# Products of 512 columns over both parts of a split activation, joined by accumulating transfers

## The chip, the cores and the metric

The kernel is one program on one core of a Trainium2 chip. The metric is the device time in microseconds (us). A measurement is the median of several runs. Beside them stands one execution that was profiled, and every row below is from that one.

## The reference, cut to what matters

One decoder layer over 512 tokens and 2048 features, in float32: a token mixer (a recurrent group and a differential-attention group), an output projection and a layer norm, and then the gated MLP, in which the change lies.

```python
hu = _causal_dwconv(jnp.einsum('bsd,df->bsf', x, w_up[i]), ffn_conv_w[i], ffn_conv_b[i])
g, u = jnp.split(hu, 2, axis=-1)
ffn = jnp.einsum('bsf,fd->bsd', jax.nn.gelu(g) * u, w_down[i])
```

`w_up` is 2048 x 11264: 44 tiles of 128 columns for g, 44 for u. The convolution is causal, of width 3, along the tokens, one filter for each column.

## The kernel before

**Split numbers.** TensorE multiplies in the type fp32r, which keeps fewer bits than float32. So every operand is split into a high part and a low part (`split`, lines 106 to 112: ScalarE copies the rounded high part, VectorE subtracts it), and a product is the sum of three matmuls (`mm3`, line 114): high by high, high by low, low by high.

**Pairs.** The first 4 tile pairs of the up projection (`PLAIN`) are computed plainly. Each of the other 40 is a `Pair`: one g tile and one u tile are seen as a 2 x 2 block matrix over the two halves of the features, the tokens as two halves of 256, and seven block products (`PRODUCTS`: p1, p5, p6, p2, p7, p3, p4) take the place of eight. The sums of weight blocks that they need are made by transfers that add to what stands in SBUF (`onto`, line 777, issued from GpSimd's queue) and by VectorE (lines 800 and 811). The sums of activation blocks are made once, in `forms` (line 727).

**Steps.** The loop of lines 916 to 923 counts steps; a pair's product number k (0 to 6) is its step k, and the pair after it begins 7 steps later. A step calls, for every pair in reach, `early` (evacuates an accumulator of the step before), `before` (loads, sums and splits of weights for later products: the blocks of a pair's p1, p5 and p6 are split at steps 5, 6 and 7 of the pair ahead of it), `late` (convolution, activation and the store of h to DRAM) and `product`. At a product TensorE makes 8 x 3 matmuls of 256 columns: three accumulators x, y, z of 256 columns serve the seven products, so p6 adds onto x only when `early` of step 1 has copied p1 out of it, p7 when that of step 3 has copied, p4 when that of step 5 has.

**Buffers.** `raw` tiles (weights as loaded, 4 KB for a partition) rotate through `RAW_UP` = 6 places, split weights through `W_BUFS` = 3, activations through `A_BUFS` = 62.

**Order.** The code names an engine for each operation, and a scheduler fixes the order on each engine when the program is built. On the chip each engine goes through its own order strictly: an instruction that waits holds up all behind it on that engine. The transfers that SyncE and GpSimd issue are two queues onto the same 16 DMA engines.

Of the kernel before, what the change touches and what calls it, by code (L numbers as in the profile page):

```python
# [10 lines left out]
F32 = mybir.dt.float32  # L11
F32R = mybir.dt.float32r
AF = mybir.ActivationFunctionType
ALU = mybir.AluOpType
# [33 lines left out]
NC_ = C_LQ + 4 * DH  # L48


A_BUFS = 62
T_BUFS = 12
RAW_BUFS = 3
RAW_UP = 6
W_BUFS = 3
TK = 0.65
LAG = 5.0
# [19 lines left out]
def f32(ap):  # L77
    return ap.bitcast(F32)
# [3 lines left out]
def trunk_kernel(ctx, tc, xT, w_qkg, w_v, gate_w, w_out0, w_out, w_up0, w_up, w_down, consts, out):  # L82
# [11 lines left out]
    def bank():  # L94
        return psum.tile([P, S], F32, tag="ps", bufs=8, name="ps")

    def a_tile(dt=F32R, name="a"):
        return act.tile([P, S], dt, tag="a", bufs=A_BUFS, name=name)

    def t_tile(dt=F32, name="t"):  # L100
        return tmp.tile([P, S], dt, tag="t", bufs=T_BUFS, name=name)
# [4 lines left out]
    def split(src, hi=None, lo=None, mk=a_tile):  # L106

        hi = mk(F32R, "hi") if hi is None else hi
        lo = mk(F32R, "lo") if lo is None else lo
        nc.scalar.activation(hi, src, AF.Copy)  # L110
        nc.vector.tensor_tensor(lo, src, f32(hi), ALU.subtract)  # L111
        return hi, lo

    def mm3(ps, w, x, first, last, onto=False):

        for n, (a, b) in enumerate(((w[0], x[0]), (w[0], x[1]), (w[1], x[0]))):
            nc.tensor.matmul(  # L117
                ps, a, b, start=first and n == 0, stop=last and n == 2, skip_group_check=onto
            )


# [432 lines left out]
    class Norm:  # L554
# [13 lines left out]
        def add(self, j, y, tok=slice(0, S), eng=nc.gpsimd):  # L568

            zs, qs = self.zs[:, tok], self.qs[:, tok]  # L570
            if j == 0:
                nc.scalar.activation(qs, y, AF.Square)
                eng.tensor_copy(zs, y)
            else:
                sq = t_tile(F32, "sq")[:, tok]
                nc.scalar.activation(sq, y, AF.Square)
                (nc.vector if j == KT - 2 else eng).tensor_tensor(zs, zs, y, ALU.add)  # L577
                eng = nc.vector if j == KT - 2 else nc.gpsimd
                eng.tensor_tensor(qs, qs, sq, ALU.add)
# [116 lines left out]
    def sides(z):  # L696
        return z[:, :HALF], z[:, HALF:]
# [29 lines left out]
    def forms(j):  # L727
        a, b = ys[j], ys[j + KT // 2]
        sub = nc.gpsimd.tensor_tensor
        t14, t23 = t_tile(F32, "t14"), t_tile(F32, "t23")  # L730
        (t1, t4), (t2, t3) = sides(t14), sides(t23)
        (b11, b12), (b21, b22) = sides(a), sides(b)
        sub(t1, b12, b11, ALU.subtract)
        sub(t2, t1, b22, ALU.subtract)
        sub(t4, t2, b21, ALU.add)
        sub(t3, b22, b12, ALU.subtract)
        h14, l14 = a_tile(F32R, "hi"), a_tile(F32R, "lo")
        nc.scalar.activation(h14, t14, AF.Copy, scale=-1.0)
        nc.vector.scalar_tensor_tensor(l14, t14, -1.0, f32(h14), ALU.mult, ALU.subtract)
        h23, l23 = split(t23)  # L740
        form["p1", j], form["p2", j] = sides(x1[j][0]), sides(x1[j + KT // 2][0])
        form["p3", j] = sides(x1[j + KT // 2][1])
        form["p5", j], form["p4", j] = zip(sides(h14), sides(l14))
        form["p6", j], form["p7", j] = zip(sides(h23), sides(l23))

    def conv(t, src, ti, *ds):
        for d in ds:
# [4 lines left out]
    def tap(src, ti):  # L752
        t = t_tile(F32, "cv")
        nc.scalar.activation(t, src, AF.Identity, scale=col(C_FW + 3 * ti + 2), bias=col(C_FB + ti))
        return t
# [11 lines left out]
    class Pair:  # L767
# [49 lines left out]

        def product(self, at):
            if at == 0:
                self.x, self.y, self.z = [bank()[:, :HALF] for _ in range(3)]  # L820
            name = PRODUCTS[at]
            ps = {"p5": self.y, "p3": self.y, "p2": self.z}.get(name, self.x)
            new = name in ("p1", "p5", "p2")
            hi, lo = self.w.pop(name)
            n = KT // 2
            for j in range(n):
                c = slice(j * P, (j + 1) * P)
                mm3(ps, (hi[:, c], lo[:, c]), form[name, j], new and j == 0, j == n - 1, not new)

        def early(self, at):  # L830
            copy, add = nc.scalar.activation, nc.vector.tensor_tensor
            a, b = slice(0, HALF), slice(HALF, S)
            if at == 1:
                self.cg = a_tile(F32, "cg")
                copy(self.cg[:, a], self.x, AF.Copy)
            elif at == 2:
                self.p5 = t_tile(F32, "p5")[:, :HALF]
                copy(self.p5, self.y, AF.Copy)
            elif at == 3:
                copy(self.cg[:, b], self.x, AF.Copy)  # L840
            elif at == 4:
                add(self.cg[:, a], self.cg[:, a], self.z, ALU.add)
            elif at == 5:
                self.cu = a_tile(F32, "cu")
                copy(self.cu[:, b], self.x, AF.Copy, scale=-1.0)
            elif at == 6:
                add(self.cg[:, b], self.cg[:, b], self.y, ALU.add)
                add(self.cu[:, b], self.cu[:, b], self.p5, ALU.subtract)
            elif at == 7:
                copy(self.cu[:, a], self.x, AF.Copy, scale=-1.0)  # L850

        def late(self, at):
            if at == 6:
                self.g = tap(self.cg, 2 * self.i)
                conv(self.g, self.cg, 2 * self.i, 1)
            elif at == 7:
                conv(self.g, self.cg, 2 * self.i, 2)
                self.u = tap(self.cu, 2 * self.i + 1)
            elif at == 8:
                conv(self.u, self.cu, 2 * self.i + 1, 1)  # L860
            elif at == 9:
                nc.scalar.activation(self.g, self.g, AF.Gelu_apprx_tanh)
            elif at == 10:
                conv(self.u, self.cu, 2 * self.i + 1, 2)
            elif at == 11:
                nc.vector.tensor_tensor(self.g, self.g, self.u, ALU.mult)
            elif at == 12:
                nc.sync.dma_start(hidd[self.i], self.g)

    pairs = [Pair(i) for i in range(PLAIN, FT)]  # L870
# [2 lines left out]
    def step(k, what, *reach):  # L873
        for n, pair in enumerate(pairs):
            if k - NP * n in range(*reach):
                getattr(pair, what)(k - NP * n)
# [39 lines left out]
    for k in range(last):  # L916
        step(k, "early", 1, 8)
        step(k, "before", -6, 5)
        step(k, "late", 6, 13)
        step(k, "product", 0, NP)  # L920
        ready({last - 5: 4, last - 3: 12, last - 2: 16}.get(k, 0))
        if k == last - 4:
            W.load()
    for k in range(last, last + 6):
        step(k, "early", 1, 8)
        step(k, "late", 6, 13)

    def down_blocks():
        while True:
# [155 lines left out]
```

## Time and profile before

| | us |
|---|---|
| median of 3 runs (2112.39 to 2113.21) | 2112.53 |
| the profiled execution | 2112.73 |
| its span, first to last instruction | 2111.0 |

The span is the stretch in which the profile shows instructions; 1.7 us of the execution lie around it. The profile's page gives the busy time of each engine; a busy TensorE (PE) is not TensorE at its best, since its matmuls are pipelined and overlap in the rows: what counts is the distance from one start to the next. Pairs are told by the copies of line 835, one for each of the 40.

### The profile page before, as it was taken

Reading aid. Unit: us, or ns where it says so; the run is one execution under the profiler, and the core shown is the slowest. Engines: PE = TensorE matmul, PEld = TensorE weight load, DVE = VectorE, ACT = ScalarE, POOL = GpSimd, SP = SyncE. Lnnn points to the kernel's source line nnn. Section 1 sums busy time; section 2 is a strip of 40 time slices with the busy share of each in tenths; the row PEclk is TensorE's granted clock in tenths of the full one; section 3 lists DMA queues with packets and bytes.
Section 4 is the critical chain, followed back from the end, with each engine's and each line's share of the span. In section 5 each row is a group of like instructions: output and inputs, shape, how many; then the busy total and the mean of one; then the engine's idle time right before and its main releaser. Section 6 shows DMA issues by size and latency. Waiting matters only on the chain.

```text
span 2111.0 us, 32632 instructions
## 1 busy us (share of the span) xinstructions
PE 2076.4 (98%) x13035; PEld 1882.6 (89%) x13035; DVE 1334.6 (63%) x2005; ACT 1004.4 (48%) x1644; POOL 240.7 (11%) x289
## 2 busy tenths in 40 slices
PE   9999999999999999999999999999999999999994
PEld 7888888888888899999999999999998888888894
DVE  6576635777335877777777777787776322443368
ACT  4475736666223645555555555555555222322144
POOL 1000000000222340000000000000000000010025
PEclk9999999999999999999999999999999999999997
DMA  6222222222433535666666666666669422333312
GB/s 217 95 80 85 81 95 71 85 98 93 152 118 120 180 86 156 170 167 173 169 175 167 168 175 171 167 175 165 171 163 329 161 93 97 125 110 100 100 50 81
DMA packets 92921, 286.67 MB, mean 136 GB/s; under 512 B 10080, under 2 KB 14176, under 8 KB 92768
## 3 DMA queue, kind: packets, MB, share of 16 engines
q1 hardware_dynamic: 81248, 242.63, 34.5%
q0 software_dynamic: 11520, 41.95, 11.1%
q8 instruction: 102, 1.67, 0.3%
q14 instruction: 51, 0.42, 0.1%
HBM read 264.62 MB, written 19.92 MB: 135 GB/s over the span
## 4 chain that ended last, share of the span: by engine, by line
PE 93%; DVE 4%; ACT 3%; issue 0%; DMA 0%; ACTq 0%; DVEq 0%
PE ps L117 91%; DVE acc L607 1%; PE ps L346 1%; PE ps L347 0%; ACT gt L455 0%; DVE acc L608 0%; PE ps L585 0%; PE ps L376 0%; DVE rstd L604 0%; DVE zs L577 0%; ACT s L358 0%; DVE y L607 0%; DVE y L608 0%; ACT a L461 0%; ACT L473 0%
## 5 line engine op out<-in xcount | busy, mean ns | idle before, releaser
L110 ACT ACTIVATE whi<-raw 128x512 fp32r<-128x512 f32 (+1 forms) x676 | 528.5, 804 | 900.4 <-PE ps L117 812.7
L111 DVE TENSOR_TENSOR wlo<-raw,whi 128x512 fp32r<-128x512 f32 (+1 forms) x676 | 614.3, 925 | 470.5 <-ACT whi L110 468.2
L117 PE MATMUL ps<-hi,whi 128*128 128x512 f32 (+1 forms) x2688 | 910.6, 339 | 0.0
L117 PE MATMUL ps<-hi,wlo 128*128 128x512 f32 (+1 forms) x2688 | 908.1, 338 | 1.2 <-DVE wlo L111 1.2
L117 PE MATMUL ps<-lo,whi 128*128 128x512 f32 (+1 forms) x2688 | 907.6, 338 | 0.0
L117 PEld LDWEIGHTS ps<-hi,wlo 128*128 128x128 f32 x2688 | 510.2, 190 | 56.1 <-DVE wlo L111 2.4
L117 PEld LDWEIGHTS ps<-hi,whi 128*128 128x128 f32 x2688 | 510.3, 190 | 53.1 <-ACT hi L110 0.3
L117 PEld LDWEIGHTS ps<-lo,whi 128*128 128x128 f32 x2688 | 510.4, 190 | 52.8 <-issue 0.5
L117 PE MATMUL ps<-x,whi 128*128 128x256 f32 x2176 | 396.9, 283 | 0.0
L117 PEld LDWEIGHTS ps<-x,whi 128*128 128x128 f32 x2176 | 339.5, 192 | 0.0
L117 PE MATMUL ps<-x,wlo 128*128 128x256 f32 x1088 | 308.0, 283 | 0.0
L117 PEld LDWEIGHTS ps<-x,wlo 128*128 128x128 f32 x1088 | 208.9, 192 | 0.0
L780 POOL DMA_DIRECT2D raw<-in_w_up x80 | 69.2, 964 | 767.8 <-DMA raw<-in_w_up 538.9
L956 POOL TENSOR_TENSOR acc<-acc,shift 128x512 f32<-128x512 f32 x16 | 23.5, 1478 | 437.7 <-ACT shift L566 296.6
L949 DVE SCALAR_TENSOR_TENSOR acc<-acc,ps 128x512 f32<-128x512 f32 x32 | 22.0, 687 | 66.7 <-PE ps L117 66.7
L748 DVE SCALAR_TENSOR_TENSOR cv<-cg,cst,cv 128x511 f32<-128x511 f32 x80 | 59.8, 747 | 1.4
L748 DVE SCALAR_TENSOR_TENSOR cv<-cu,cst,cv 128x511 f32<-128x511 f32 x80 | 59.5, 744 | 0.0
L117 PE MATMUL ps<-x,hi 128*128 128x256 f32 x256 | 49.4, 294 | 5.1 <-DVE x L111 3.3
L117 PE MATMUL ps<-hi 128*128 128x256 f32 (+1 forms) x176 | 51.9, 295 | 0.0
L117 PE MATMUL ps<-lo,hi 128*128 128x256 f32 (+1 forms) x176 | 51.5, 293 | 0.0
L117 PE MATMUL ps<-hi,lo 128*128 128x256 f32 (+1 forms) x176 | 51.5, 293 | 0.0
L800 DVE TENSOR_TENSOR raw<-raw 128x1024 f32<-128x1024 f32 x40 | 49.0, 1226 | 3.1 <-DMA raw<-in_w_up 1.8
(198 smaller groups left out, 1899.8 us busy)
## 6 DMA issues: line engine op xcount, KB each, us to landing
raw<-in_w_up SPq DMA_DIRECT2D x176, 512.0 KB, 4.1
raw<-in_w_down SPq DMA_DIRECT2D x88, 512.0 KB, 3.3
raw<-in_w_up POOLq DMA_DIRECT2D x80, 512.0 KB, 7.1
raw<-in_w_qkg SPq DMA_DIRECT2D x64, 512.0 KB, 3.5
raw<-in_w_out SPq DMA_DIRECT2D x32, 512.0 KB, 3.6
hidd<-cv SPq DMA_DIRECT2D x44, 256.0 KB, 4.2
hid<-hidd SPq DMA_DIRECT2D x44, 256.0 KB, 5.4
raw<-in_w_v SPq DMA_DIRECT2D x15, 512.0 KB, 4.3
```

What stands on the lines that cost most here:

```text
L110: nc.scalar.activation(hi, src, AF.Copy)
L111: nc.vector.tensor_tensor(lo, src, f32(hi), ALU.subtract)
L117: nc.tensor.matmul(ps, a, b, start=first and n == 0, stop=last and n == 2, skip_group_check=onto)
L346: nc.tensor.matmul(ps[:, :L], qs, k[c][:, :L], start=True, stop=False)
L607: sub.tensor_tensor(y, y, self.m[:, tok], ALU.subtract)
L748: nc.vector.scalar_tensor_tensor(t[:, d:], src[:, : S - d], col(C_FW + 3 * ti + 2 - d), t[:, d:], ALU.mult, ALU.add)
L780: nc.gpsimd.dma_start(self.raw[name], w_up[2 * (self.i - 2) + g][:, n * 1024 : (n + 1) * 1024], accum_op=ALU.add,)
L800: add(s2, self.raw["r21"], self.raw["r11"], ALU.add)
L949: nc.vector.scalar_tensor_tensor(acc[dt], acc[dt], 1.0 if c else ALPHA, ps, ALU.mult, ALU.add)
L956: nc.gpsimd.tensor_tensor(acc[d], acc[d], norm2.c, ALU.subtract)
```

## The change

A pair's matmul with a high half of weights now takes the high and the low part of the activation side by side, as one operand of 512 columns, and leaves high-by-high in the first 256 columns of the accumulator and high-by-low in the second (`mm2`). The matmul with the low half of weights adds onto the first 256 columns. So a block takes two matmuls, and the accumulators are 512 columns wide. `early` copies and adds at 512 columns, into `cg` and `cu` tiles of 1024 columns that have a ring of 3 of their own. Where a tile is complete, at steps 6 and 7, a transfer from GpSimd's queue adds its second half to its first (`accum_op=ALU.add`, SBUF to SBUF, 2 KB for a partition). `late` begins two steps later and reads the sum. `RAW_UP` goes from 6 to 5 and `A_BUFS` from 62 to 60. `forms` splits four quarters where it split two halves.

```diff
-A_BUFS = 62
+A_BUFS = 60
-RAW_UP = 6
+RAW_UP = 5
+    def mm2(ps, w, x, first, last, onto=False):
+        n = ps.shape[-1] // 2
+        steps = [(ps, w[0], x), (ps[:, :n], w[1], x[:, :n])]
+        for k, (o, a, b) in enumerate(reversed(steps) if last else steps):
+            nc.tensor.matmul(
+                o, a, b, start=first and k == 0, stop=last and k == 1, skip_group_check=onto
+            )
...
-        h14, l14 = a_tile(F32R, "hi"), a_tile(F32R, "lo")
-        nc.scalar.activation(h14, t14, AF.Copy, scale=-1.0)
-        nc.vector.scalar_tensor_tensor(l14, t14, -1.0, f32(h14), ALU.mult, ALU.subtract)
-        h23, l23 = split(t23)
+        for name, t in (("p5", t1), ("p4", t4)):
+            z = form[name, j] = a_tile(F32R, "hl")
+            hi, lo = sides(z)
+            nc.scalar.activation(hi, t, AF.Copy, scale=-1.0)
+            nc.vector.scalar_tensor_tensor(lo, t, -1.0, f32(hi), ALU.mult, ALU.subtract)
+        for name, t in (("p6", t2), ("p7", t3)):
+            form[name, j] = a_tile(F32R, "hl")
+            split(t, *sides(form[name, j]))
...
-                self.x, self.y, self.z = [bank()[:, :HALF] for _ in range(3)]
+                self.x, self.y, self.z = bank(), bank(), bank()
...
-                mm3(ps, (hi[:, c], lo[:, c]), form[name, j], new and j == 0, j == n - 1, not new)
+                mm2(ps, (hi[:, c], lo[:, c]), form[name, j], new and j == 0, j == n - 1, not new)
...
+            two = lambda z: z.rearrange("p (z t) -> p z t", z=2)
+            x, y, z = [two(k) for k in (self.x, self.y, self.z)]
             if at == 1:
-                self.cg = a_tile(F32, "cg")
-                copy(self.cg[:, a], self.x, AF.Copy)
+                self.cg = W.pool.tile([P, 2 * S], F32, tag="c", bufs=3, name="cg")
+                self.g2 = two(self.cg)
+                copy(self.g2[:, :, a], x, AF.Copy)
...
             elif at == 6:
-                add(self.cg[:, b], self.cg[:, b], self.y, ALU.add)
-                add(self.cu[:, b], self.cu[:, b], self.p5, ALU.subtract)
+                add(self.g2[:, :, b], self.g2[:, :, b], y, ALU.add)
+                nc.gpsimd.dma_start(self.cg[:, :S], self.cg[:, S:], accum_op=ALU.add)
+                add(self.u2[:, :, b], self.u2[:, :, b], self.p5, ALU.subtract)
             elif at == 7:
-                copy(self.cu[:, a], self.x, AF.Copy, scale=-1.0)
+                copy(self.u2[:, :, a], x, AF.Copy, scale=-1.0)
+                nc.gpsimd.dma_start(self.cu[:, :S], self.cu[:, S:], accum_op=ALU.add)
...
-            if at == 6:
-                self.g = tap(self.cg, 2 * self.i)
+            if at == 8:
+                self.g = tap(self.cg[:, :S], 2 * self.i)
+            elif at == 9:
                 conv(self.g, self.cg, 2 * self.i, 1)
-            elif at == 7:
+            elif at == 10:
                 conv(self.g, self.cg, 2 * self.i, 2)
-                self.u = tap(self.cu, 2 * self.i + 1)
+                self.u = tap(self.cu[:, :S], 2 * self.i + 1)
```

The scheduler's order on the engines, in the middle of the pairs. First GpSimd's queue. Before, it holds nothing but the two sums of weights of each pair, one after the other.

```order
L780 DMA raw_14346<-in_w_up 128x1024
L780 DMA raw_14515<-in_w_up 128x1024
L780 DMA raw_14580<-in_w_up 128x1024
L780 DMA raw_14749<-in_w_up 128x1024
L780 DMA raw_14814<-in_w_up 128x1024
```

In the changed kernel (where `onto` is line 792) a pair has four transfers: the sum onto the next pair's r21 (raw_10518), the sum onto its r11 (raw_10569), and then this pair's `cg` and `cu`.

```order
L792 DMA raw_10518<-in_w_up 128x1024
L792 DMA raw_10569<-in_w_up 128x1024
L865 DMA cg_10512<-cg_10512 128x512
L869 DMA cu_10615<-cu_10615 128x512
L792 DMA raw_10698<-in_w_up 128x1024
L792 DMA raw_10749<-in_w_up 128x1024
L865 DMA cg_10692<-cg_10692 128x512
L869 DMA cu_10795<-cu_10795 128x512
```

So the transfer that completes `cg` stands right behind the sum onto the next pair's r11, which waits until p1's block of that pair has been split out of the same tile.

Next ScalarE around the tap of g (line 754 before, 766 after: the first term of the convolution and its bias). Before, the tap of `cg` has only VectorE's addition ahead of it, and the copy that frees x for p6 (line 835, `cg_11701<-ps`) comes six instructions later.

```order
L110 ACTIVATE whi_11633<-raw_11473 128x1024
L754 ACTIVATE cv_11637<-cg_11467,cst_78 128x512
L110 ACTIVATE whi_11667<-raw_11603 128x1024
L850 ACTIVATE cu_11597<-ps_11440 128x256
L862 ACTIVATE cv_11637<-cv_11637 128x512
L754 ACTIVATE cv_11672<-cu_11597,cst_78 128x512
L110 ACTIVATE whi_11703<-raw_11540 128x1024
L835 ACTIVATE cg_11701<-ps_11674 128x256
```

In the changed kernel the tap waits for the transfer of `cg`, and the copy out of x (now line 851) stands right behind it.

```order
L110 ACTIVATE whi_10643<-raw_10518 128x1024
L868 ACTIVATE cu_10615<-ps_10493 128x2x256
L110 ACTIVATE whi_10668<-raw_10621 128x1024
L766 ACTIVATE cv_10702<-cg_10512,cst_78 128x512
L851 ACTIVATE cg_10692<-ps_10673 128x2x256
L110 ACTIVATE whi_10694<-raw_10571 128x1024
L854 ACTIVATE p5_10720<-ps_10674 128x512
L110 ACTIVATE whi_10723<-raw_10569 128x1024
```

The tap has moved from ahead of the split of p6's block (whi_11667) to behind it (whi_10668), and the copy that lets p6 begin (L851) is now the next instruction behind the tap.

Last VectorE over the same stretch. Before, from the addition that completes `cg` (line 847) on:

```order
L847 TENSOR_TENSOR cg_11467<-cg_11467,ps_11441 128x256
L111 TENSOR_TENSOR wlo_11634<-raw_11473,whi_11633 128x1024
L748 SCALAR_TENSOR_TENSOR cv_11637<-cg_11467,cst_78,cv_11637 128x511
L748 SCALAR_TENSOR_TENSOR cv_11637<-cg_11467,cst_78,cv_11637 128x510
L111 TENSOR_TENSOR wlo_11668<-raw_11603,whi_11667 128x1024
L811 TENSOR_TENSOR raw_11603<-raw_11603,raw_11540 128x1024
L748 SCALAR_TENSOR_TENSOR cv_11672<-cu_11597,cst_78,cv_11672 128x511
```

In the changed kernel, from the first convolution step behind the tap on (the numbers are those of ScalarE's rows above; line 760 is the convolution, 823 and 812 are the sums of weights, 858 adds z to `cg`):

```order
L760 SCALAR_TENSOR_TENSOR cv_10702<-cg_10512,cst_78,cv_10702 128x511
L823 TENSOR_TENSOR raw_10621<-raw_10621,raw_10571 128x1024
L111 TENSOR_TENSOR wlo_10695<-raw_10571,whi_10694 128x1024
L760 SCALAR_TENSOR_TENSOR cv_10702<-cg_10512,cst_78,cv_10702 128x510
L111 TENSOR_TENSOR wlo_10724<-raw_10569,whi_10723 128x1024
L760 SCALAR_TENSOR_TENSOR cv_10754<-cu_10615,cst_78,cv_10754 128x511
L760 SCALAR_TENSOR_TENSOR cv_10754<-cu_10615,cst_78,cv_10754 128x510
L885 TENSOR_TENSOR cv_10702<-cv_10702,cv_10754 128x512
L111 TENSOR_TENSOR wlo_10746<-raw_10621,whi_10745 128x1024
L858 TENSOR_TENSOR cg_10692<-cg_10692,ps_10675 128x2x256
L812 TENSOR_TENSOR raw_10801<-raw_10698,raw_10749 128x1024
L111 TENSOR_TENSOR wlo_10774<-raw_10666,whi_10773 128x1024
```

The next three rows there are the subtraction of p5 from `cu` (L866, 128x2x256), the split of the next pair's p1 (L111, wlo_10798<-raw_10749) and the addition that completes this pair's `cg` (L864). What moved: the convolution's first step, which waits for the transfer of `cg`, now stands ahead of a whole pair's work on VectorE, whose end releases the next such transfer.

## Rows read from the trace of the kernel before

**Rows 1.** Page, part 1: busy time, share of span, count by engine.
```profile
PE 2076.4 (98%) x13035; PEld 1882.6 (89%) x13035; DVE 1334.6 (63%) x2005; ACT 1004.4 (48%) x1644; POOL 240.7 (11%) x289
```

**Rows 2.** Stretch in the pairs: busy us (instructions) by engine, clock, DMA share, GB/s.
```profile
1200.00:1400.00 200.00, 200.00 (x1669) 200.00 (x1669) 153.90 (x169) 105.70 (x148) 17.27 (x20) 1.00 0.65 170
```

**Rows 3.** Tile cg: one line's executions, ns min/median/max, first and last start.
```profile
L835 ACT ACTIVATE cg<-ps x40: 362/365/367, 793.5 to 1579.7; 128x256 f32<-128x256 f32 x40
```

**Rows 4.** Timeline of TensorE: start us, duration us; 256 columns, then 512.
```profile
1200.06 0.28 PE L117 MATMUL ps<-lo,whi 128*128 128x256 f32 x1
1200.18 0.28 PE L117 MATMUL ps<-hi,wlo 128*128 128x256 f32 x1
...
1595.13 0.39 PE L117 MATMUL ps<-hi,whi 128*128 128x512 f32 x1
...
1598.98 0.39 PE L117 MATMUL ps<-hi,wlo 128*128 128x512 f32 x1
```

**Rows 5.** Timeline of VectorE, from the split of a next pair's p1 on.
```profile
1208.31 1.23 DVE L111 TENSOR_TENSOR wlo<-raw,whi 128x1024 fp32r<-128x1024 f32 x1 [1.65 <-ACT whi L110]
1209.46 0.42 DVE L848 TENSOR_TENSOR cu<-cu,p 128x256 f32<-128x256 f32 x1
...
1215.40 1.23 DVE L811 TENSOR_TENSOR raw<-raw 128x1024 f32<-128x1024 f32 x1
1216.54 0.74 DVE L748 SCALAR_TENSOR_TENSOR cv<-cu,cst,cv 128x511 f32<-128x511 f32 x1
1217.20 1.22 DVE L111 TENSOR_TENSOR wlo<-raw,whi 128x1024 fp32r<-128x1024 f32 x1
1218.34 0.74 DVE L748 SCALAR_TENSOR_TENSOR cv<-cu,cst,cv 128x510 f32<-128x510 f32 x1
1219.11 0.69 DVE L866 TENSOR_TENSOR cv<-cv 128x512 f32<-128x512 f32 x1
1219.84 1.23 DVE L111 TENSOR_TENSOR wlo<-raw,whi 128x1024 fp32r<-128x1024 f32 x1
```

**Rows 6.** Page, part 5: a VectorE operation of 512 columns on an accumulator.
```profile
L949 DVE SCALAR_TENSOR_TENSOR acc<-acc,ps 128x512 f32<-128x512 f32 x32 | 22.0, 687 | 66.7 <-PE ps L117 66.7
```

**Rows 7.** Timeline of ScalarE in the same pair.
```profile
1207.22 1.06 ACT L110 ACTIVATE whi<-raw 128x1024 fp32r<-128x1024 f32 x1 [1.82 <-PE ps L117]
...
1211.07 0.80 ACT L754 ACTIVATE cv<-cg,cst 128x512 f32<-128x512 f32 x1
...
1214.27 0.62 ACT L862 ACTIVATE cv<-cv 128x512 f32<-128x512 f32 x1
```

**Rows 8.** Timeline of GpSimd: transfers issued, two pairs.
```profile
1209.84 1.73 POOL L780 DMA_DIRECT2D raw<-in_w_up  x2 [18.43 <-DVE wlo L111]
1229.99 0.86 POOL L780 DMA_DIRECT2D raw<-in_w_up  x1 [18.43 <-DMA raw<-in_w_up]
1231.68 0.85 POOL L780 DMA_DIRECT2D raw<-in_w_up  x1 [0.83 <-issue]
```

**Rows 9.** Transfers issued at 1229.99, 1231.68, 1203.81, 1212.45 us: KB, us to landing.
```profile
raw<-in_w_up POOLq DMA_DIRECT2D x1, 512.0 KB, 5.2
...
raw<-in_w_up POOLq DMA_DIRECT2D x1, 512.0 KB, 8.3
...
raw<-in_w_up SPq DMA_DIRECT2D x1, 512.0 KB, 3.2
...
raw<-in_w_up SPq DMA_DIRECT2D x1, 512.0 KB, 8.1
```

**Rows 10.** Page, part 3: queue, packets, MB, share of 16 engines' span.
```profile
q0 software_dynamic: 11520, 41.95, 11.1%
```

**Rows 11.** Stretches around the one clock drop ahead of the last 30 us.
```profile
696.00:700.00 4.00, 2.24 (x19) 2.04 (x18) 4.00 (x6) 2.40 (x5) 4.00 (x6) 1.00 0.16 58
700.00:703.00 3.00, 0.74 (x6) 0.54 (x5) 3.00 (x4) 3.00 (x9) 3.00 (x5) 0.99 0.50 185
703.00:706.00 3.00, 1.97 (x9) 1.97 (x10) 3.00 (x6) 2.00 (x4) 1.57 (x2) 0.50 0.00 0
```

More of the change, by code (lines that the diff above doesn't have):

```diff
@@ L736, in forms @@
         sub(t3, b22, b12, ALU.subtract)
-        h14, l14 = a_tile(F32R, "hi"), a_tile(F32R, "lo")
-        nc.scalar.activation(h14, t14, AF.Copy, scale=-1.0)
-        nc.vector.scalar_tensor_tensor(l14, t14, -1.0, f32(h14), ALU.mult, ALU.subtract)
-        h23, l23 = split(t23)
[L741 to L744, printed above, removed]
+        form["p1", j], form["p2", j] = x1[j][0], x1[j + KT // 2][0]
+        form["p3", j] = x1[j + KT // 2][1]
+        for name, t in (("p5", t1), ("p4", t4)):
[6 more added lines that the diff above has]
+            split(t, *sides(form[name, j]))
     def conv(t, src, ti, *ds):
@@ L833, in early @@
             if at == 1:
-                self.cg = a_tile(F32, "cg")
-                copy(self.cg[:, a], self.x, AF.Copy)
+                self.cg = W.pool.tile([P, 2 * S], F32, tag="c", bufs=3, name="cg")
+                self.g2 = two(self.cg)
+                copy(self.g2[:, :, a], x, AF.Copy)
             elif at == 2:
-                self.p5 = t_tile(F32, "p5")[:, :HALF]
-                copy(self.p5, self.y, AF.Copy)
+                self.p5 = two(t_tile(F32, "p5"))
+                copy(self.p5, y, AF.Copy)
@@ L839, in early @@
             elif at == 3:
-                copy(self.cg[:, b], self.x, AF.Copy)
+                copy(self.g2[:, :, b], x, AF.Copy)
             elif at == 4:
-                add(self.cg[:, a], self.cg[:, a], self.z, ALU.add)
+                add(self.g2[:, :, a], self.g2[:, :, a], z, ALU.add)
             elif at == 5:
-                self.cu = a_tile(F32, "cu")
-                copy(self.cu[:, b], self.x, AF.Copy, scale=-1.0)
+                self.cu = W.pool.tile([P, 2 * S], F32, tag="c", bufs=3, name="cu")
@@ L846, in early @@
+                self.u2 = two(self.cu)
+                copy(self.u2[:, :, b], x, AF.Copy, scale=-1.0)
             elif at == 6:
-                add(self.cg[:, b], self.cg[:, b], self.y, ALU.add)
-                add(self.cu[:, b], self.cu[:, b], self.p5, ALU.subtract)
+                add(self.g2[:, :, b], self.g2[:, :, b], y, ALU.add)
+                nc.gpsimd.dma_start(self.cg[:, :S], self.cg[:, S:], accum_op=ALU.add)
+                add(self.u2[:, :, b], self.u2[:, :, b], self.p5, ALU.subtract)
@@ L857, in late @@
                 conv(self.g, self.cg, 2 * self.i, 2)
-                self.u = tap(self.cu, 2 * self.i + 1)
-            elif at == 8:
+                self.u = tap(self.cu[:, :S], 2 * self.i + 1)
+            elif at == 11:
                 conv(self.u, self.cu, 2 * self.i + 1, 1)
-            elif at == 9:
                 nc.scalar.activation(self.g, self.g, AF.Gelu_apprx_tanh)
-            elif at == 10:
+            elif at == 13:
                 conv(self.u, self.cu, 2 * self.i + 1, 2)
-            elif at == 11:
+            elif at == 14:
@@ L866, in late @@
                 nc.vector.tensor_tensor(self.g, self.g, self.u, ALU.mult)
-            elif at == 12:
+            elif at == 15:
                 nc.sync.dma_start(hidd[self.i], self.g)
@@ L918, in trunk_kernel @@
         step(k, "before", -6, 5)
-        step(k, "late", 6, 13)
+        step(k, "late", 8, 16)
         step(k, "product", 0, NP)
@@ L923, in trunk_kernel @@
             W.load()
-    for k in range(last, last + 6):
+    for k in range(last, last + 9):
         step(k, "early", 1, 8)
-        step(k, "late", 6, 13)
+        step(k, "late", 8, 16)
     def down_blocks():
```

## The prediction

> **What bounds the kernel now.** I read the engines' busy shares first, then the stretches, then the timelines of the engines in the pairs. TensorE is busy for 98% of the span [rows 1], and in the 200 us from 1200 on for all of them, at full clock (1.00, 2.4 GHz), while VectorE has 154 of 200 us and ScalarE 106 [rows 2]. The copy out of p1 starts first at 793.5 and last at 1579.7 us: 786.2 us for 39 distances, 20.16 us a pair [rows 3]. A matmul of 256 columns starts 0.120 us after the one before it [rows 4], and 7 products x 24 matmuls x 0.120 are 20.16 us. So a pair costs exactly its matmuls; nothing else shows.
>
> **What TensorE is spared.** Matmuls of 512 columns start 0.2265 us apart: 3.85 us for 17 distances, 1595.13 to 1598.98 [rows 4]. A block now costs 0.2265 + 0.120 = 0.3465 us where it cost 0.360, a product 2.77 us where it cost 2.88, a pair 19.40 us where it cost 20.16. That is 0.0135 us for each of 40 x 56 = 2240 blocks, 30 us in all, if TensorE stays the bound. That 512 and 256 columns alternate is not in the trace; the two distances are 256/2.4 and 512/2.4 ns plus the same 13 ns, so I add them up unchanged.
>
> The Trainium skill gives another price: its page "TensorE: Matmul & The Clock Gate" (Back-to-back issue gap) puts the isolated distance at the columns over 2.4 GHz plus some 2.5 ns, by which a matmul less would spare an estimated 2.5 x 2240 = 6 us. The rows show 13 ns where it has 2.5.
>
> **What is laid on the other engines.** Copies and additions of accumulators go from 256 to 512 columns. An addition from an accumulator is 0.69 us at 512 [rows 6]; three of them were 0.42 [rows 5], so VectorE gains 0.8 us a pair. ScalarE's five copies go to about the 0.62 us of a 512-column pass [rows 7], 1.3 us a pair. Both engines have the room as totals [rows 2]. Each matmul taken away also takes its weight load, which lies beside other matmuls. The four splits in `forms`, the scheduler's changed order in the attention, and two `a` tiles less I cost at nothing: TensorE covers them as it covers their likes now, and an engine that runs out there would cost a few us at most. One `raw` place less lets the loads of r11 and r12 start only when p2's and p7's blocks have been split, some three steps (8 us) ahead of their use; a load from SyncE lands in 3.2 us when alone [rows 9]. Hidden. So is the store of h, three steps later than now: only the down projection reads it.
>
> **The loop that the transfer of `cg` closes.** Here lies the cost. The order on the engines puts these in a ring, each waiting for the one before:
>
> 1. The tap of g on ScalarE waits for `cg` to land: 0.1 us of hand-over (my estimate; between VectorE and ScalarE rows show 0.03, to GpSimd 0.3), and 0.80 us itself [rows 7].
> 2. VectorE's first convolution step waits for the tap, and behind it, in order, stand 13 more operations up to the split of the next pair's p1. By distances between starts: four convolution steps at 0.66 (followed by another kind) to 0.77 (followed by what reads it), the product 0.73, the sum of weights and the splits 1.14 to 1.15, all from [rows 5]; two operations of 512 columns at 0.65, a little under the 0.69 of [rows 6]. That is 0.66 + 0.66 + 0.75 + 0.77 + 0.73 + 5 x 1.14 + 0.09 (the last split to its end) + 2 x 1.15 + 2 x 0.65 = 13.0 us. With every one hidden 0.09 us under the next it is 12.6, with none 13.65 (the durations added).
> 3. That split ends, and 0.30 us later (1209.54 to 1209.84, [rows 5, 8]) GpSimd issues the sum onto r11, which had waited for it. `cg`'s addition ends 0.65 us after the split, while GpSimd is still issuing, so `cg` goes out right behind.
> 4. The sum onto r11 lands 5.2 us after issue when nothing else moves [rows 9]. The load onto the next r21 goes out just then (when p5's block is split, 1.2 us after `cg`'s addition) and moves beside its end; I take 5.5, and 5.7 as the high end, both estimates.
> 5. `cg`'s transfer moves half the bytes and comes after it in the same queue. Alone: 41.95 MB of such sums took 11.1% of 16 engines' 2111 us [rows 10], 80 of them, so 2.93 us each and 1.46 for half. Sharing with a load: of two sums issued at 1229.99 and 1231.68 [rows 8] the first landed 5.2 us later and the second 8.3 [rows 9], 4.8 us after the first, half of it 2.4; or all 4.8, if the 128 rows count and not their bytes. That the two queues hold each other up shows in SyncE's load, 3.2 us alone and 8.1 beside two such sums [rows 9]. Since r21's load is about, I take 2.4.
>
> Sum: 0.1 + 0.8 + 13.0 + 0.3 + 5.5 + 2.4 = **22.1 us** around the ring, between 20.4 (0.05 + 0.8 + 12.6 + 0.3 + 5.2 + 1.46) and 25.5 (0.2 + 0.8 + 13.65 + 0.3 + 5.7 + 4.8). All of it is longer than TensorE's 19.40, and even the lower end is longer than the 20.16 of now. TensorE is drawn into it since the copy that frees x for p6 stands right behind the tap on ScalarE: it should stand still for 2.7 us ahead of every p6. The other way around, over TensorE, is shorter: tap 0.8, copy 0.6, p6, p2 and p7 8.3, copy 0.6, split 1.06 and 1.23 [rows 5, 7] come to 12.6 against 13.8. Before, the tap waited for VectorE's addition alone, and no transfer stood between the pairs' work.
>
> A pair then costs 22.1 - 20.16 = 1.94 us more, over 39 distances 76 us. At the end, the last `cu` goes through a transfer ahead of its tap, and splits for the down projection stand behind that tap on ScalarE; between 0 (hidden) and 6 us (issue to landing of such a transfer and its tap): I take 3. From the profiled execution's 2112.73, which is the median of the runs to within 0.2 us: 2112.7 + 76 + 3 = **2192 us**.
>
> **Rivals.**
>
> *The transfer of `cg` does not queue behind the sum onto r11 (faster).* Then it is issued 0.3 + 0.86 us [rows 8] after the split of p1 and lands as a sum of half the bytes would alone, 5.2 - 1.46 = 3.7 us later: 0.1 + 0.8 + 13.0 + 1.2 + 3.7 = 18.8, under 19.40, and TensorE stays the bound. 2112.7 - 30 + 3 = 2086 us. It turns at a landing 4.3 us after issue. Against it: the second of two sums never landed near the first in [rows 8, 9], though each alone takes 5.2. I give it 0.13.
>
> The Trainium skill would lean to this one: "DMA: Bandwidth & Descriptors" (Anatomy of one DMA) has 2.0 us plus the bytes over 436 GB/s for a transfer from GpSimd's queue, an estimated 2.6 us for 256 KB, and so a ring of some 18 us. By the same rule the 512 KB of [rows 9] would take 3.2 us, and they took 5.2: an adding transfer is dearer than the rule.
>
> *TensorE's clock drops in the gaps (slower still).* The one drop ahead of the end came after TensorE had been idle for 1.76 and 2.26 of 7 us, and 0.50 (1.2 GHz) was granted afterwards [rows 11]. One gap of 2.7 us in 22 is smaller, and I think the clock holds. At half the clock p6 alone would take 2.8 us more, the way over TensorE 15.4 instead of 12.6, which is 1.6 over VectorE's 13.8: 23.7 us a pair, 2254 us. With p2 slowed as well it would be 26.5 us, 2363 us. I give it 0.10.
>
> *The ring is short after all.* With every term near its low end a pair stays within 20.4 to 21.1 us, and the time within 2125 to 2152: 0.08. Within 0.2% of now 0.03, since that needs a ring between 20.0 and 20.2.
>
> **How the numbers follow.** My forecast, a ring of 21.1 to 24 us, has 0.66, and its own range is 2152 to 2265. With the short ring below it and half of the clock's case above it, 2125 to 2300 holds 8 in 10; the faster case, no change and the dearer half of the clock's case stay out. 0.2% (4 us) is about what a measurement of this kernel tells from no change. Faster 0.13, the same 0.03, slower 0.84.
>
> **What the changed profile would show.** The distance between the first and the last copy of line 851 over 39: 22.1 by me, 19.4 by the first rival. The tap of `cg` on ScalarE idle ahead of it, released by a transfer, in every pair; TensorE idle ahead of p6, released by that copy; GpSimd's `cg` issues landing 7 to 8 us after issue (under 4.3 by the rival); VectorE without idle time from the convolution to the split of p1. Starts of matmuls 0.227 and 0.120 us apart show the relief. I am wrong if the tap finds `cg` landed, or if another instruction than the tap starts the wait.

## The result and the profile after

| | us |
|---|---|
| changed kernel, median of 4 runs (2212.78 to 2218.88) | 2215.52 |
| kernel before, median of 4 runs (2111.99 to 2113.21) | 2112.46 |
| ratio, 95% interval | 1.0488 [1.047, 1.0506] |
| the profiled execution and its span | 2212.78, 2210.9 |

The change costs 103 us, where 79 were forecast; between the two profiled executions it is 100.1, since the profiled execution of the changed kernel is its fastest. The page of the changed kernel, part 1, answers to [rows 1]: TensorE has 2240 matmuls less and is busy for 95% instead of 98%.

```profile
PE 2093.0 (95%) x10795; PEld 1780.0 (81%) x10795; DVE 1348.5 (61%) x2021; ACT 1045.9 (47%) x1660; POOL 309.1 (14%) x369
```

The stretch of [rows 2]: TensorE has 184 of 200 us instead of 200, and the mean clock is no longer 1.00. VectorE does less in 200 us than before (142 us for 154), since fewer pairs pass; ScalarE does as much (105 us), since each of its copies is longer.

```profile
1200.00:1400.00 200.00, 183.56 (x1004) 157.65 (x1005) 141.79 (x153) 105.04 (x135) 31.09 (x36) 0.97 0.72 175
```

The tile `cg` in the changed kernel, as in [rows 3]: first the executions of the copy of line 851 and of the tap, then what the instructions on `cg` waited for and who waited for them (us, times), then the transfers' time to landing.

```profile
L851 ACT ACTIVATE cg<-ps x40: 574/576/601, 793.8 to 1674.4; 128x512 f32<-128x512 f32 x40
...
  DMA cg<-cg: 183.1, 39
...
  DVE cv L760: 171.2, 40
...
  PE ps L127: 78.6, 39
...
DMA to landing us min/median/max: 6.6/7.5/9.7
```

From 793.8 to 1674.4 are 880.6 us over 39 distances: 22.58 us a pair, 2.42 more than before, 94.4 in all. Behind the last copy the span has 536.5 us where it had 531.3, 5.2 more. With 0.3 us at the start that is the 100 us. And the three waits form a chain: the tap waits for the transfer in 39 pairs, VectorE's convolution for the tap, TensorE for the copy behind the tap, 2.0 us each time (78.6 over 39).

One pair follows, engine by engine. ScalarE's timeline (start us, duration us, in brackets the idle time and what ended it):

```profile
1222.64 0.81 ACT L766 ACTIVATE cv<-cg,cst 128x512 f32<-128x512 f32 x1 [4.08 <-DMA cg<-cg]
1223.36 0.58 ACT L851 ACTIVATE cg<-ps 128x512 f32<-128x512 f32 x1
...
1244.84 0.81 ACT L766 ACTIVATE cv<-cg,cst 128x512 f32<-128x512 f32 x1 [4.93 <-DMA cg<-cg]
```

VectorE's timeline; the first two rows are of the pair before it, the rest of this one, to compare with [rows 5]:

```profile
1212.01 0.69 DVE L866 TENSOR_TENSOR cu<-cu,p 128x512 f32<-128x512 f32 x1 [0.37 <-ACT cu L862]
1212.96 1.23 DVE L111 TENSOR_TENSOR wlo<-raw,whi 128x1024 fp32r<-128x1024 f32 x1 [0.25 <-ACT whi L110]
...
1223.49 0.75 DVE L760 SCALAR_TENSOR_TENSOR cv<-cg,cst,cv 128x511 f32<-128x511 f32 x1 [3.66 <-ACT cv L766]
...
1235.07 1.22 DVE L111 TENSOR_TENSOR wlo<-raw,whi 128x1024 fp32r<-128x1024 f32 x1
1236.21 0.68 DVE L864 TENSOR_TENSOR cg<-cg,ps 128x512 f32<-128x512 f32 x1
```

GpSimd's issues in the same pair, as in [rows 8], the sum onto the next r11 first and `cg` behind it:

```profile
1236.58 0.86 POOL L792 DMA_DIRECT2D raw<-in_w_up  x1 [12.42 <-DVE wlo L111]
1237.18 1.14 POOL L865 DMA_DIRECT2D cg<-cg  x1
```

And the landing of these two, KB and us from issue, as in [rows 9]:

```profile
raw<-in_w_up POOLq DMA_DIRECT2D x1, 512.0 KB, 5.5
...
cg<-cg POOLq DMA_DIRECT2D x1, 256.0 KB, 7.6
```

The reader can walk the ring: tap to convolution 0.85 us (1222.64 to 1223.49), VectorE without a gap to the end of the split of p1 at 1236.29, which is 12.80, 0.29 to GpSimd's issue at 1236.58, 5.5 to the landing of the sum, and `cg` at 1237.18 + 7.6 = 1244.8, 2.7 behind it; the next tap starts at 1244.84. Together 22.20 us, with TensorE and ScalarE waiting in turn.

### The profile page after: what moved, and what is told of

It reads as the page before. It is cut to its first block, busy times and chain, and to the rows that moved or that the text cites. A ratio compares the mean times of both kernels' runs of the same rounds, so it can differ in the third digit from the quotient of the medians.

```text
span 2210.9 us, 28573 instructions
## 1 busy us (share of the span) xinstructions
PE 2093.0 (95%) x10795; PEld 1780.0 (81%) x10795; DVE 1348.5 (61%) x2021; ACT 1045.9 (47%) x1660; POOL 309.1 (14%) x369
## 4 chain that ended last, share of the span: by engine, by line
PE 52%; DMA 21%; issue 13%; DVE 8%; ACT 4%; POOL 1%; POOLq 0%; ACTq 0%; DVEq 0%; SPq 0%
PE ps L117 50%; DMA cg<-cg 13%; DMA raw<-in_w_up 8%; DVE wlo L111 3%; ACT cv L766 1%; DVE raw L823 1%; POOL raw L792 1%; PE ps L127 1%; DVE acc L617 1%; PE ps L356 1%; ACT gt L465 0%; PE ps L357 0%; DVE acc L618 0%; PE ps L595 0%; ACT s L368 0%
## 5 line engine op out<-in xcount | busy, mean ns | idle before, releaser
L111 DVE TENSOR_TENSOR wlo<-raw,whi 128x512 fp32r<-128x512 f32 (+1 forms) x676 | 611.8, 922 | 415.1 <-ACT whi L110 413.7
L127 PE MATMUL ps<-hl,whi 128*128 128x512 f32 x1280 | 489.2, 414 | 78.6 <-ACT cg L851 78.6
L117 PE MATMUL ps<-hi,whi 128*128 128x512 f32 (+1 forms) x1408 | 548.6, 390 | 0.8 <-ACT hi L110 0.7
L117 PE MATMUL ps<-hi,wlo 128*128 128x512 f32 (+1 forms) x1408 | 545.9, 388 | 3.4 <-DVE wlo L111 3.4
L117 PE MATMUL ps<-lo,whi 128*128 128x512 f32 (+1 forms) x1408 | 545.5, 387 | 0.9 <-DVE lo L111 0.9
L127 PEld LDWEIGHTS ps<-hl,whi 128*128 128x128 f32 x1280 | 251.2, 196 | 138.1 <-ACT cg L851 90.9
L127 PE MATMUL ps<-x,whi 128*128 128x512 f32 x960 | 349.2, 398 | 0.0
L127 PE MATMUL ps<-hl,wlo 128*128 128x256 f32 x1280 | 343.0, 289 | 0.0
L117 PEld LDWEIGHTS ps<-hi,wlo 128*128 128x128 f32 x1408 | 264.4, 188 | 59.2 <-DVE wlo L111 5.3
L117 PEld LDWEIGHTS ps<-hi,whi 128*128 128x128 f32 x1408 | 264.5, 188 | 53.7 <-ACT hi L110 1.6
L127 PEld LDWEIGHTS ps<-hl,wlo 128*128 128x128 f32 x1280 | 252.5, 197 | 13.4
L968 DVE SCALAR_TENSOR_TENSOR acc<-acc,ps 128x512 f32<-128x512 f32 x32 | 21.9, 685 | 65.7 <-PE ps L117 65.7
```

The source lines that it names most:

```text
L117: nc.tensor.matmul(ps, a, b, start=first and n == 0, stop=last and n == 2, skip_group_check=onto)
L127: nc.tensor.matmul(o, a, b, start=first and k == 0, stop=last and k == 1, skip_group_check=onto)
L968: nc.vector.scalar_tensor_tensor(acc[dt], acc[dt], 1.0 if c else ALPHA, ps, ALU.mult, ALU.add)
```

## The experiments

Each was compared with the kernel before; ratios are to it. "A pair" is the distance between the first and the last of the 40 copies out of p1, over 39. The twelve were not planned at once: the second four follow from what the first showed, the last four from the second.

**1. Neither part nor transfer** (`e_none`).

```diff
-                nc.gpsimd.dma_start(self.cg[:, :S], self.cg[:, S:], accum_op=ALU.add)
-                nc.gpsimd.dma_start(self.cu[:, :S], self.cu[:, S:], accum_op=ALU.add)
```

> Both SBUF-to-SBUF transfers are left out, so the products of the weights' high halves with the low parts of x1 are missing from the output; all else stays as in the changed kernel. If the ring of tap, VectorE chain, sum onto r11 and transfer of cg sets the pair's time, it is gone: TensorE is the bound at 19.40 us a pair, no gap ahead of p6, full clock, 2083 to 2088 us. If the 512-column copies and additions, the rawu pool of five places or the alternation of 512 and 256 columns cost something of their own, that part stays: a pair above 19.6 us, and the time above 2092 us. If the alternation gives no relief at all, 20.16 us a pair and 2112 us.

2105.63 us, 0.9968 [0.9958, 0.9979], 19.79 us a pair:

```profile
L851 ACT ACTIVATE cg<-ps x40: 598/598/602, 795.1 to 1567.1; 128x512 f32<-128x512 f32 x40
```

The ring is gone, and with it the gaps of 2 us and the drops of the clock within the pairs. Five places for raw weights, wider copies and wider additions cost next to nothing here: TensorE stands idle for 0.04 us a pair. But the relief is smaller than forecast: 0.37 us a pair, not 0.76. Nor does the end get all of it: behind the last copy are 539.0 us, 7.7 more than before.

**2. The transfers are issued, and nobody reads what they add** (`e_unread`).

```diff
-                self.g = tap(self.cg[:, :S], 2 * self.i)
+                self.g = tap(self.cg[:, S:], 2 * self.i)
...
-                self.u = tap(self.cu[:, :S], 2 * self.i + 1)
+                self.u = tap(self.cu[:, S:], 2 * self.i + 1)
```

(`conv` reads the same half. This half is what the transfer takes from: it holds high-by-low alone. So what the output lacks here, and in experiment 6, is the first half, high-by-high and low-by-high, and not the low parts' products, as the two expectations have it. The waits are those that they describe.)

> Both transfers are issued as in the changed kernel, but the taps and convolutions read the other half of cg and cu (the source of the transfer), so nobody waits for a landing except for the place in the pool; the low parts' products are missing from the output. By the ring it is the waiting that costs: 2083 to 2090 us, 19.4 to 19.6 us a pair, as without transfers. By the rival that the transfers' traffic costs (it holds up the loads of weights in the other queue, and the splits with them), it stays above 2150 us. In between, 2095 to 2150, both have a part.

2192.08 us, 1.0379 [1.0364, 1.0395], 21.91 us a pair. Read by itself this says that the waiting for `cg` is not the cause, and that the rival is right. The trace names another wait. VectorE's timeline, where line 812 is the addition of r21 and r11:

```profile
1045.89 1.23 DVE L812 TENSOR_TENSOR raw<-raw 128x1024 f32<-128x1024 f32 x1 [5.07 <-issue]
...
1050.51 1.22 DVE L111 TENSOR_TENSOR wlo<-raw,whi 128x1024 fp32r<-128x1024 f32 x1
...
1066.86 1.23 DVE L812 TENSOR_TENSOR raw<-raw 128x1024 f32<-128x1024 f32 x1 [1.78 <-issue]
```

The load onto the next r21 (SyncE, issued at 1051.76) and the sum onto it (GpSimd, 1059.51), KB and us to landing:

```profile
raw<-in_w_up SPq DMA_DIRECT2D x1, 512.0 KB, 7.2
...
raw<-in_w_up POOLq DMA_DIRECT2D x1, 512.0 KB, 7.3
```

This is a second ring. A pair takes five raw tiles (r21, r11, r12, s2, r22), and with five places the next r21 gets the place of this one. It is free when p5's block is split out of it, at 1051.73; the load lands at 1058.9, the sum is issued at 1059.51 and lands at 1066.8, the addition starts at 1066.86, and 5.8 us later the next split of p5 ends. That is 21.0 us around, above the 19.7 that TensorE needs. The mean of 21.9 holds more than this pair: 15 of the 39 distances hold a stretch at half the clock and are 24.47 us on average, the other 24 are 20.31. How the excess divides between the ring and the clock that its gaps cost is not shown.

**3. No sum onto r11** (`e_no11`).

```diff
                 add(s2, self.raw["r21"], self.raw["r11"], ALU.add)
-                self.onto("r11", (1, 0))
```

> The sum onto r11 is left out, so p7's weights are those of one block alone and the output differs there; cg's transfer is then first in GpSimd's queue when it is issued. If cg is late because it queues behind the sum onto r11, it lands 3.5 to 4.5 us after issue instead of 7.5, the ring is 18.8 to 19.6 us, and the time 2083 to 2095 us. If an adding transfer of 256 KB is slow by itself whatever stands ahead of it, it lands after 6 us or more, the ring stays at 21 us or more, and the time above 2150 us.

2105.43 us, 0.9967 [0.9954, 0.998], 19.78 us a pair. The transfers of `cg` in this run:

```profile
DMA to landing us min/median/max: 3.6/3.6/7.6
```

An adding transfer of 256 KB lands 3.6 us after issue when it is first in the queue, and 7.5 behind a sum of 512 KB. So the ring over `cg` is the queue's doing. The time missed the expected 2083 to 2095 us by the smaller relief alone. The second ring opened as well: the load and the sum of r21, beside `cg` and `cu` but with no sum onto r11, now took

```profile
raw<-in_w_up SPq DMA_DIRECT2D x1, 512.0 KB, 4.0
...
raw<-in_w_up POOLq DMA_DIRECT2D x1, 512.0 KB, 5.5
```

where they had taken 7.2 and 7.3.

**4. `cg` added by VectorE, `cu` by its transfer** (`e_vcg`).

```diff
-                nc.gpsimd.dma_start(self.cg[:, :S], self.cg[:, S:], accum_op=ALU.add)
+                add(self.cg[:, :S], self.cg[:, :S], self.cg[:, S:], ALU.add)
```

> cg's two parts are added by VectorE (one addition of 512 columns, some 0.65 us a pair), cu's by the transfer as in the changed kernel. The ring runs over cg alone, so by it this version is bound by TensorE: 19.4 to 19.6 us a pair, 2084 to 2092 us, faster than the kernel before by 1%. If cu's transfer closes a ring of its own (its tap stands ahead of other copies on ScalarE), the pair stays above 20.5 us and the time above 2125 us.

2155.46 us, 1.0201 [1.0164, 1.0239], 20.73 us a pair in the profiled execution, which is the fastest of four from 2145 to 2165 us. It is a miss, since the expectation had one ring only in its first case. VectorE's addition of r21 and r11 is the late one here too: it waited 22 times between 900 and 1500 us, 48 us in all.

**5. Both added by VectorE** (`e_vec`): the same edit for `cu`.

> Both parts are added by VectorE (two additions of 512 columns, 0.69 us each as the run with one showed, 1.4 us a pair) and no transfer is left. The run without either part or transfer took 19.8 us a pair. If the transfers' waits and traffic are what costs, VectorE's extra work fits beside TensorE: 19.8 us a pair and 2104 to 2110 us, a little faster than the kernel before. If the additions lengthen the way from the sum onto r21 over VectorE's addition and splits to the next load onto its place, the pair stays above 20.2 us and the time above 2120 us.

2145.09 us, 1.0159 [1.0143, 1.0174], 20.67 us a pair. Without any transfer between the pairs the kernel is still slower than before: the second ring has VectorE's work in it, and the two additions lengthen it by what experiment 1 had to spare and more. VectorE's addition of r21 and r11 waited 29 times between 900 and 1500 us, 81 us in all.

**6. As 2, with six places for raw weights** (`e_unread_r6t10`).

```diff
-T_BUFS = 12
+T_BUFS = 10
-RAW_UP = 5
+RAW_UP = 6
```

> As the run in which nobody waits for the transfers (the low parts' products are missing), with six places for raw weights instead of five, for which two of the twelve t places are given up. That run took 21.9 us a pair: VectorE's addition of r21 and r11 waited for the sum onto r21, and this for the load of r21, 7 us each beside the transfers, and the load for its place. If it is the place that closes this second ring, a sixth opens it: 19.8 to 20.2 us a pair, 2104 to 2120 us. If it is the traffic alone that makes loads late, the pair stays above 21 us and the time above 2150 us.

2105.29 us, 0.9964 [0.9953, 0.9976]. The copies out of p1, 19.74 us a pair:

```profile
L851 ACT ACTIVATE cg<-ps x40: 598/599/601, 794.6 to 1564.4; 128x512 f32<-128x512 f32 x40
```

One place takes 87 us away, with all four transfers of a pair still running, and the clock falls in none of the 39 distances. The second ring is the place's doing.

**7. The changed kernel with six places** (`a_r6t10`): the edit of 6 alone.

> The changed kernel with six places for raw weights instead of five (and ten t places instead of twelve); nothing is left out. If the ring over cg's transfer is the longer of the two rings and stands by itself, it stays at 22.0 to 22.6 us a pair and the time at 2185 to 2220 us. If the place taken away were the cause, the time would fall to 2105 to 2130 us.

2234.29 us, 1.0575 [1.0554, 1.0597], 23.00 us a pair. The ring over `cg` stands without the other. It is longer than expected, and I only partly know why: 21 of the 39 pairs hold a drop of the clock here, 14 in the changed kernel (these 21 are 23.4 us on average, the others 22.5), and with a sixth place the scheduler has the sum onto the next r21 go out right behind `cg`, whose landing takes 7.8 us instead of 7.5.

**8. The kernel before, with the transfers' traffic** (`b_dummy`).

```diff
                 add(self.cg[:, b], self.cg[:, b], self.y, ALU.add)
+                nc.gpsimd.dma_start(spare[0], self.cg, accum_op=ALU.add)
...
                 copy(self.cu[:, a], self.x, AF.Copy, scale=-1.0)
+                nc.gpsimd.dma_start(spare[1], self.cu, accum_op=ALU.add)
```

> The kernel before, with two transfers a pair more on GpSimd's queue: cg and cu, when complete, are added onto two spare tiles that nobody reads (ten t places remain for the rest). Traffic alone, with nobody waiting and six places for raw weights. By the two rings, both of which need a wait or a fifth place, it changes nothing: 20.16 us a pair and 2112 to 2118 us. If traffic alone makes the weights late, the pair goes above 20.6 us and the time above 2130 us.

2114.57 us, 1.0008 [0.9998, 1.0017], 20.16 us a pair. These transfers land in 7.3 and 8.1 us, as late as in the changed kernel (7.5 and 6.8), and cost nothing clear of noise where nobody waits and there are six places.

**9. Both added by VectorE, six places** (`e_vec_r6`): the edits of 5 and 6.

> Both parts are added by VectorE and there are six places for raw weights (ten t places); nothing is left out. Neither of the two rings is left: no transfer that the tap waits for, and the load onto r21 one place earlier. So 19.8 us a pair as in the runs without a ring, full clock, and 2103 to 2110 us, 0.2 to 0.4% faster than the kernel before. If VectorE's 1.4 us more a pair run it out, the pair stays above 20.2 us and the time above 2118 us.

2108.14 us, 0.998 [0.9971, 0.9989], 19.74 us a pair: it beats both kernels, by 0.2% the one before. The stretch of [rows 2] has TensorE at all of its 200 us again, at full clock, with VectorE at 174:

```profile
1200.00:1400.00 200.00, 200.00 (x1137) 173.87 (x1136) 174.06 (x193) 120.42 (x153) 17.10 (x20) 1.00 0.69 174
```

**10. The same with earlier loads for the down projection** (`e_vec_r6_early`).

```diff
-        ready({last - 5: 4, last - 3: 12, last - 2: 16}.get(k, 0))
         if k == last - 4:
             W.load()
+        if k == last - 2:
+            W.load(6)
+        ready({last - 5: 4, last - 3: 8, last - 2: 10}.get(k, 0))
```

> The same, with the first weights of the down projection loaded ahead of most of the tiles of h, and fewer of these (10 instead of 16) asked for before the last product. In the runs without a ring the stretch from the last copy of a pair to the end was 539 us, where it was 531.3 before: TensorE waited 5.4 us for splits of these weights and ran 3.4 us at half the clock. If their loads' place in SyncE's queue is the cause, 3 to 7 us are saved and the time is 2097 to 2104 us; if VectorE's own load at the end is, it is the same as without, within 2 us.

2106.55 us, 0.9971 [0.9961, 0.9982]. Behind the last copy 541.0 us against 542.6 in 9; the gaps there are 3.7 and 2.2 us instead of 1.8 and 7.6, with the clock down for as long. The difference to 9 lies within the intervals: the loads' place is not the main cause, and what makes the end 8 to 11 us longer than before stays open.

**11. `cg` by VectorE, `cu` by its transfer, six places** (`e_vcg_r6`): the edits of 4 and 6.

> cg's parts added by VectorE, cu's by the transfer, with six places for raw weights; nothing is left out. With five places it was 20.7 us a pair. If what was left there was the ring over r21's place, a sixth place ends it: 19.8 to 20.0 us a pair, 2103 to 2112 us. If cu's transfer closes a ring of its own (with six places the order has the addition of r21 and r11 right behind the convolution that waits for cu's tap), the pair stays above 20.5 us and the time above 2130 us.

2226.54 us, 1.0543 [1.0526, 1.056], 22.72 us a pair. With six places the sums onto the next r11 and the next r21 both stand ahead of `cu`, which lands third (issued at 1015.02; KB, us):

```profile
cu<-cu POOLq DMA_DIRECT2D x1, 256.0 KB, 10.9
```

ScalarE's timeline shows who stands behind it:

```profile
1002.55 0.81 ACT L766 ACTIVATE cv<-cu,cst 128x512 f32<-128x512 f32 x1 [4.65 <-DMA cu<-cu]
1003.27 0.57 ACT L856 ACTIVATE cg<-ps 128x512 f32<-128x512 f32 x1
...
1014.12 0.60 ACT L868 ACTIVATE cu<-ps 128x512 f32<-128x512 f32 x1 [0.52 <-PE ps L127]
```

The tap of `cu` holds the copy that frees x for p7; p7, p3 and p4 end at 1014.1; the copy out of p4 completes the next `cu`, whose transfer lands at 1025.9. A third ring, over TensorE, of 23.3 us in this pair, in which TensorE ran at half the clock between 1005.5 and 1008.6 us.

**12. The changed kernel without the product of g and u** (`e_noprod`).

```diff
-                nc.vector.tensor_tensor(self.g, self.g, self.u, ALU.mult)
```

> The changed kernel without the product of g and u (g alone is stored, so the output is not the reference's): VectorE has 0.7 us less in its chain from the convolution to the split of the next p1. If this chain is part of the ring that sets the pair, the pair falls by 0.7 us, from 22.58 to 21.9 us (the second ring, over r21's place, holds it at some 21.9 too), and the time to 2185 to 2192 us. If VectorE's work is not on the way, since VectorE is idle for a third of the time, nothing changes: 2210 to 2220 us.

2186.53 us, 1.035 [1.0335, 1.0366], 22.02 us a pair:

```profile
L851 ACT ACTIVATE cg<-ps x40: 573/575/601, 794.1 to 1652.9; 128x512 f32<-128x512 f32 x40
```

That is 0.56 less, and the time is where it was expected. The clock falls in 9 of the 39 distances here and in 14 in the changed kernel; those without a drop are 21.69 us on average against 22.35, 0.66 less, about the 0.69 of the product. VectorE is idle for some 30% of the time, and yet 0.69 us taken from it shortens the pair.

## Why the prediction was right, and where its sizes were off

**The ring.** Forecast 22.1 us a pair, measured 22.58. Step 1, hand-over and tap: 0.06 + 0.85 for 0.9. Step 2, VectorE's chain: 12.80 in the pair shown for 13.0, and 12 shows that it is on the way. (Its low end is 12.5 by the terms given, 13.65 less 13 times 0.09, and not 12.6.) Step 3: 0.29 for 0.3. Step 4, the sum onto r11: 5.5 as forecast. Step 5, `cg` behind it: 2.7 for 2.4. Experiment 3 shows that this step decides: first in the queue, `cg` lands 3.6 us after issue, for the 3.7 of the first rival, and the pair is bound by TensorE. That rival had the transfer's duration right; its condition, no queueing, is what failed.

The Trainium skill's "DMA: Bandwidth & Descriptors" (Anatomy of one DMA) gives 2.0 us plus bytes over 436 GB/s, an estimated 2.6 us for 256 KB. The measured 3.6 us is an adding transfer's, and behind another one the rule does not tell the landing at all: 7.5 and 10.9 us were measured.

**The clock.** I wrote that it would hold, and that step failed. Granted clock and starts of line 851 together: 14 of the 39 distances hold a stretch at 0.50 (1.2 GHz), and these are 22.98 us on average, the other 25 are 22.35. By this comparison of averages 0.63 x 14 = 9 of the 94 us are the clock's, and the ring without it is 0.25 us from the forecast. The stretches of one such pair of the changed kernel, around the tap at 1199.73 (columns: PE busy, clock, DMA share, GB/s):

```profile
1199.00:1201.88 2.88, 0.96 (x5) 1.00 0.59 127
1201.88:1205.30 3.42, 3.42 (x14) 0.50 0.78 119
1205.30:1222.60 17.30, 17.30 (x98) 1.00 0.75 198
```

TensorE was idle for 1.92 us ahead of p6, and 3.4 us at half the clock followed. The rival in the prediction priced a slowed p6 at 23.7 us in every pair. Here the first two rows of VectorE's timeline above show what it did: VectorE waits 0.37 and 0.25 us, together 0.62, for ScalarE's work behind late matmuls, and the next pair's tap comes 22.91 us after this one's. So the mechanism of that rival was there, in a third of the pairs and at a smaller price.

**The relief.** Forecast 0.0135 us a block and 30 us, measured 0.0075 and 17. Experiment 9, without a ring, shows the starts of two 512-column matmuls four blocks apart (TensorE's timeline):

```profile
1005.08 0.40 PE L127 MATMUL ps<-hl,whi 128*128 128x512 f32 x1
...
1006.49 0.40 PE L127 MATMUL ps<-hl,whi 128*128 128x512 f32 x1
```

1.41 us for four blocks is 0.3525 each, and 56 of them are the 19.74 us a pair; I had added 0.2265 and 0.120. The two lengths in turn do not keep the distances that each has among its like [rows 4]. Since the ring was the bound this did not reach the result, but the first rival's 2086 us was out of reach: 2105 was measured.

**The exit.** Forecast 3 us of 0 to 6, measured 5.2. That this lies in the range is luck: I put it down to the transfer of the last `cu`, and without any transfer (1) the exit is 7.7 us longer than before. There TensorE waits 5.4 us for splits of the down projection's weights; what makes the exit longer stays open, as 10 found.

**What was costed at nothing.** The engines' added work was hidden, as said. The place for raw weights was not: I reasoned on the loads of r11 and r12. In step 4 I let the load onto the next r21 go out when p5's block is split, but did not follow it around: the next r21 gets the place of this one, and the load, the sum onto it and VectorE's work up to the split of p5 lie between. Five places make it 21.9 us a pair beside the transfers' traffic (2), and 20.7 without transfers when VectorE has more to do (5); with neither, they cost nothing (1). The place does not show in the changed kernel's time, since the ring over `cg` is longer (7). The likeliest case was therefore right for the reason given, and one step of it, "Hidden", was right by luck, since something worse stood ahead of it.

**Bandwidth.** The rival of the experiments, that the traffic itself costs, falls with 6 and 8. It does make loads late, 7.2 us for 4.0 beside one sum of 512 KB more (2, 3), but that costs only where a ring waits for them. The Trainium skill's "DMA: Bandwidth & Descriptors" (Queues, rings and completion order) says that a transfer's completion is written only after all earlier writes of the same DMA engine, across its queues; the loads that land late beside sums agree with it, though no run here tells this from sharing the engines' time.

## What to carry to other kernels

Ask of every new wait not how long the transfer takes alone but which ring it closes: what must end before the transfer is issued, what stands ahead of it in its queue, and whether this in turn waits for what the transfer releases. An engine that is idle for 30% of the time can still be on such a ring throughout. And where removing the suspected wait leaves the time nearly as it was, look for a second ring of almost the same length before giving the theory up: here, ending the wait for the transfers alone (2) bought 23 us, the sixth place alone (7) bought nothing, and both together (6) bought 110.

## What the runs showed of the hardware

- Adding transfers on GpSimd's queue landed one behind the other: 256 KB took 3.6 us from issue when first (3), 7.5 behind one sum of 512 KB (the changed kernel), 10.9 behind two (11), each the median of 40.
- A plain load of 512 KB from SyncE's queue, 3.2 us alone [rows 9], took 4.0 beside `cg` and `cu` (3) and 7.2 beside these and a sum of 512 KB (2).
- Matmuls of 512 and of 256 columns in turn (fp32r, full granted clock) took 0.3525 us for the two, 6 ns more than the distances among their like add up to.
- In the changed kernel, where TensorE stood still for 2.0 us on average ahead of p6, the granted clock fell to 0.50 in 14 of the 39 distances, for 3.4 us in the pair shown. In the runs without these gaps (1, 3, 6, 9) it fell nowhere between the first pair and the last; the next drop came behind them, where TensorE waited for the down projection's first weights.
